# A hybrid decoder layer on one core: conditioning in whole, evenly spaced visits, and an instruction order planned by a simulated timeline

## The chip, the cores and the metric

The kernel runs on one core of one Trainium2 chip. The metric is device time in microseconds (us) of one execution. The times of before are 1353.8, 1354.12 and 1354.7 us, with a median of 1354.12.

TensorE (PE in the profile; PEld is its loading of weights), VectorE (DVE), ScalarE (ACT) and GpSimd (POOL) each run their own instructions in order. SyncE (SP) issues nearly all loads from HBM, one after another in its own order.

## The reference

One decoder layer works on 256 prompt tokens of one request and on 8 requests of 4 sample tokens, 288 columns in all, of width D = 2048. Everything is fp32.

```
mod = silu(c) @ w_ada + b_ada            # one row per request: sh1, sc1, g1, sh2, sc2, g2
h = rmsnorm(x, norm1) * (1 + sc1) + sh1
u_pool, z, xbc, dt = split(h @ w_in)     # 512, 1536, 2560, 24
pool_out = pool_mixer(u_pool)            # trailing means over 2, 4, 8, 16 tokens, a linear map each
ssd_out = ssd_mixer(z, xbc, dt)          # causal conv, chunked scan over 24 heads, gate silu(z), norm
x = x + g1 * (concat(pool_out, ssd_out) @ w_out)
h = rmsnorm(x, norm2) * (1 + sc2) + sh2
gate, val = split(h @ w_up)              # 5504 each
x = x + g2 * ((silu(causal_conv3(gate)) * val) @ w_down)
y = rmsnorm(x, norm_f)
```

The outputs are y and the states (pool, conv, SSD, feed-forward) of both groups.

## The kernel before, in words

**Projections.** Activations lie transposed: 128 rows of features, 288 columns of tokens. Each 128x128 block of a weight is multiplied in three matmuls of 288 columns (lines 303, 304, 305): the high part of the weight by the high and by the low part of the activation, and the low part of the weight by the high part. The weights are fp32 in HBM. They come as chunks of mostly 512 KB into tiles named raw_... (`load`, line 270, on SP's queue). ScalarE casts the high part (whi, line 289), VectorE subtracts it to get the low part (wlo, line 291), and only then can the chunk's matmuls run.

**Stages.** (1) Up to about 18 us: the sums of squares of x, and the first group of the conditioning. (2) The xbc projection, in seven blocks of k-tiles and output columns (`BLOCKS`), so that work begins before all of the input's modulation is known. Between its chunks come *visits* of the conditioning for the first norm, groups g1 to g5 (matmul line 378, tiles raw_ada and adag): each computes the shift and scale of some k-tiles. A visit's result is copied by ScalarE (asb), transposed on TensorE (adat) and added to the bias by VectorE. (3) From about 185 us: the last xbc block, then the uz projection (the z and pool columns). Between its matmuls come the SSD and pooling work (conv, cumulative sums cse, cb, state products s and yo, the outputs y; generators pulled as `back`) and parts 2, 3 and 4 of the conditioning (g1, sh2, sc2). (4) The out projection (mm_out and mm_outp) with the residual and the squares for the second norm. (5) The second norm (ssum2, rstd2), the first up columns (mm_up), then 40 pairs of gate and val columns and the down projection; part 5 of the conditioning (g2) lies at its start. (6) The last norm and the stores of y.

**Conditioning in parts.** Part p is a product of the 9 conditioning rows, padded to 32, with a 2048x2048 piece of w_ada. `ada_part_units` loads two chunks per k-tile and issues two matmuls of 512 columns for each (line 332; the profile counts two passes for one such fp32 matmul). It yields after every chunk or every few. The loops of stages 3 and 4 advance it with `pull(adas, rate)` at fixed rates (`RA1`, `RA2`, `TA`, `ADA_OUT`, divided by `AY`), so that as a rule four chunks, eight program matmuls, come together.

**What sets the order.** The code is written with the framework's tile scheduler. It takes the instructions with their priorities (`tc.high_priority()`), tile buffers, and pins (`tc.keep_in_program_order`), and decides in which order they stand on each engine and queue, the loads on SP too. A stretch inside `in_order` (the beginning) keeps the written order. The raw tiles rotate through slots kept by the class `_W`: 8 in pool w0 and 8 in pool w1, all shared by conditioning and projections; w0 is dropped ahead of the last xbc block. `top_up` issues loads of the early stage ahead, as many as there are slots.

**Norms.** `final_sum` adds the last column sums (ssum2, line 241), ScalarE takes the square root and VectorE the reciprocal (r3rstd2, lines 247 and 248), TensorE spreads it over the partitions (pbrstd2, line 254), ScalarE copies it, VectorE and GpSimd modulate x, and ScalarE casts the first operand h2h for mm_up. The SSD output has the same chain as ysum and pbrstdy. In the order of before, matmuls of part 5 (`GA`) and of part 4 lie between the links.

**Other loads.** vec (constants per feature, 476 KB) is issued on SP when block 4 of xbc starts, the pool weights poolw (256 KB) in `late_loads`, and the SSD's old states h0 (profile rows h<-h) in the SSD part.

Of the kernel before, what the change touches and what calls it, by code (L numbers as in the profile page):

```python
# [12 lines left out]
F32 = mybir.dt.float32  # L13
# [26 lines left out]
RAW0, RAW1, RAW2 = 8, 8, 1  # L40
# [11 lines left out]
AY = 2  # L52

RA1, RA2, RB1, RB2, RB3 = 0.5, 0.4, 1.0, 1.0, 1.0
TA, ADA_OUT = 4, 4
# [109 lines left out]
def kernel(ctx: ExitStack, tc, ins, outs):  # L165
# [101 lines left out]
    def load(key):  # L267
        off, cols = S.items[key]
        t = wp[0].tile([P, RAWC], F32, tag="raw", name="raw_" + "_".join(map(str, key)))
        nc.sync.dma_start(t[:, :cols], wflat[off:off + P * cols].rearrange("(p n) -> p n", p=P))  # L270
        return t
# [5 lines left out]
    def top_up():  # L277

        while queue and nloads[0] - min((n for n, _ in ahead.values()), default=nloads[0]) < RAW0 + RAW1:
            key = queue.popleft()  # L280
            ahead[key] = (nloads[0], load(key))
            nloads[0] += 1
# [121 lines left out]

    def ada_part_units(part, ay=1):
# [8 lines left out]
        yield  # L414
        pt = ada_tr(asb, 512, f"p{part}")
        for i in range(4):
            o = ada[:, part].rearrange("p (j i) c -> p j i c", j=4)[:, :, i, :]
            b = bada[:, part].rearrange("p (j i) -> p j i", j=4)[:, :, i]
            src = pt[:, i * P:(i + 1) * P].rearrange("p (j c) -> p j c", j=4)[:, :, 0:NC9]
            nc.vector.tensor_tensor(o, src, b.unsqueeze(2).to_broadcast([P, 4, NC9]), ALU.add)  # L420
        if part == 4:
            ada_scale(1, 4, vec[:, V_N2:V_N2 + KT], 0, KT)
        yield
# [33 lines left out]
    class _W:  # L457


        def __init__(self):  # L460
            self.slots = {"raw": [], "whi": [], "wlo": []}
            self.i = {"raw": 0, "whi": 0, "wlo": 0}

        def add(self, pool, nraw, nsp):
            for tag, n in (("raw", nraw), ("whi", nsp), ("wlo", nsp)):
                m = len(self.slots[tag])
                if m:
                    r = self.i[tag] % m
                    self.slots[tag] = self.slots[tag][r:] + self.slots[tag][:r]
                    self.i[tag] = 0  # L470
                self.slots[tag] += [(pool, n)] * n

        def drop(self, pool):
            for tag, sl in self.slots.items():
                r = self.i[tag] % len(sl)
                self.slots[tag] = [x for x in sl[r:] + sl[:r] if x[0] is not pool]
                self.i[tag] = 0

        def tile(self, shape, dt, tag, name):
            pool, n = self.slots[tag][self.i[tag] % len(self.slots[tag])]  # L480
            self.i[tag] += 1
            return pool.tile(shape, dt, tag=tag, name=name, bufs=n)

    wp[0] = _W()
    wp[0].add(ctx.enter_context(tc.tile_pool(name="w1", bufs=1, side="right")), RAW1, SPLIT1)
# [16 lines left out]
    wp[0].add(w0, RAW0, SPLIT0)  # L502
# [405 lines left out]
    adas = chain(*(ada_part_units(p, AY) for p in (2, 3, 4)))  # L908
# [86 lines left out]
    for bi in range(len(BLOCKS)):  # L995
        last = bi + 1 == len(BLOCKS)
        top_up()
        if last:

            wp[0].drop(w0)  # L1000
            w0_ctx.close()
            sx[0] = mx_ctx.enter_context(tc.tile_pool(name="sx", bufs=1, reuse_waits="tile"))
            raw = load(("dt",))[:, :KT * NH].rearrange("p (k h) -> p k h", h=NH)
# [11 lines left out]
            late_states()  # L1015
            dt_stage(ps)
# [4 lines left out]
        for i, m in enumerate(xbc_units(bi)):  # L1021
# [9 lines left out]
            else:  # L1031
                pull(back, 0.5 if m < 20 else RB1) if m >= 9 else None
                pull(adas, RA1 / AY)
# [4 lines left out]
    for m in list(range(4 + 3 * ZEARLY, 16)) + ULATE:  # L1038
        for _ in uz_units(m):
# [3 lines left out]
            pull(adas, RA2 / AY)  # L1043
# [7 lines left out]
    pull(adas, TA / AY)  # L1051
# [36 lines left out]
    for i in range(KT // YK):  # L1088
# [6 lines left out]
        if i == 3:  # L1095
            psq = aux("ysum")
            col_sums(psq, ssq, ones[:, 0:1], True, True)
            _, rstdy = rstd_of(psq, NH * 64, "rstdy")
    mx_ctx.close()
# [51 lines left out]
    for m in range(16):  # L1151
# [3 lines left out]
        if m == 5:  # L1155
            wp[0].add(w2, RAW2, SPLIT2)
        if m == 0:
            out_norm(ps0[0], m)
        else:
            for i, (pz, pp) in enumerate(out_units(m)):  # L1160
                if m == KT - 1 and i == 5:
                    all_but_last("ssum2")
                if i == NZ // YK - 1:
                    out_norm(pz, m)
        residual(ps0[1] if m == 0 else pp, 2, m)
        squares(m, "a")
        pull(adas, (1 + (m >= 14 - ADA_OUT)) / AY)
# [3 lines left out]

    adag2 = ada_part_units(5)
# [285 lines left out]
```

## Time and profile before

| what | us |
|---|---|
| median of 3 runs | 1354.12 |
| the profiled execution's own time | 1353.11 |
| its span in the trace | 1351.3 |
| TensorE busy in it | 1337.3 |
| VectorE busy | 820.0 |
| ScalarE busy | 579.4 |
| GpSimd busy | 227.5 |

The page gives busy times and, in 40 slices of the span, the busy tenths of each engine and of the DMA engines. The windows view gives the same for stretches that one chooses, with the granted TensorE clock (PEclk, 1.00 is full speed), the share of the 16 DMA engines in use and GB/s. The waits view lists what an engine waited for. The timeline lists start, duration, engine, line and tiles; neighbours of one kind are put together (x16 is sixteen passes), and durations of matmuls overlap, so that the time between two starts tells more than a duration. A row of an issue names the queue (SPq) and the chunk's tile without its numbers.

### The profile page before, as it was taken

What the parts mean: (1) busy time and instruction counts of PE and PEld (TensorE: products, weight loads), DVE (VectorE), ACT (ScalarE), POOL (GpSimd) and SP (SyncE); (2) the same over time, 40 slices, a digit from 0 to 9 for tenths busy, and PEclk for the clock granted to TensorE, in tenths of its full rate; (3) what the DMA queues carried; (4) which work ended last, traced back from release to release, by engine and by line L of the source; (5) the groups of instructions that cost most, each with busy time, mean ns of one, the idle gap of its engine ahead of it and who ended that gap; (6) DMA issues with size and microseconds to landing.
All of it is one profiled execution on the core that took longest, in us unless ns stands there. A gap on an engine that the chain in (4) does not pass through costs nothing.

```text
span 1351.3 us, 26246 instructions
## 1 busy us (share of the span) xinstructions
PE 1337.3 (99%) x10517; PEld 1247.5 (92%) x10517; DVE 820.0 (61%) x1394; ACT 579.4 (43%) x911; POOL 227.5 (17%) x449
## 2 busy tenths in 40 slices
PE   9999999999999999999999999999999999999997
PEld 8889997776789889999999999999999999999997
DVE  5776568778665568645665445656655556566543
ACT  5343244587733335434443333434433343444442
POOL 0000012122122223111211001321120011132221
PEclk9999999999999999999999999999999999999999
DMA  9999768978888877787555555655555565566531
GB/s 373 405 408 368 252 242 324 340 257 295 324 332 323 320 253 257 249 280 265 181 187 182 162 178 183 204 183 196 181 180 164 184 191 184 187 207 194 179 119 70
DMA packets 97482, 323.19 MB, mean 239 GB/s; under 512 B 10768, under 2 KB 19920, under 8 KB 97360
## 3 DMA queue, kind: packets, MB, share of 16 engines
q1 hardware_dynamic: 93600, 310.79, 66.3%
q0 software_dynamic: 3184, 9.69, 2.0%
q8 instruction: 82, 1.34, 0.4%
q10 hardware_dynamic: 576, 1.03, 0.2%
q14 instruction: 40, 0.33, 0.1%
HBM read 309.78 MB, written 10.39 MB: 237 GB/s over the span
## 4 chain that ended last, share of the span: by engine, by line
PE 74%; DVE 1%; issue 0%; ACT 0%; DVEq 0%
PE mm_down L304 7%; PE mm_down L303 7%; PE mm_down L305 7%; PE mm_gate L303 6%; PE mm_val L304 6%; PE mm_gate L304 6%; PE mm_val L305 6%; PE mm_gate L305 6%; PE mm_val L303 6%; PE adap L332 3%; PE mm_out L303 2%; PE mm_out L304 2%; PE mm_out L305 2%; PE mm_up L303 1%; PE mm_up L304 1%; PE mm_up L305 1%
## 5 line engine op out<-in xcount | busy, mean ns | idle before, releaser
L304 PE MATMUL mm_down<-al,whi_down 128*128 128x288 f32 x688 | 202.5, 294 | 0.0
L303 PE MATMUL mm_down<-ah,whi_down 128*128 128x288 f32 x688 | 202.4, 294 | 0.0
L305 PE MATMUL mm_down<-ah,wlo_down 128*128 128x288 f32 x688 | 202.0, 294 | 0.0
L304 PE MATMUL mm_val<-h2l,whi_val 128*128 128x288 f32 x640 | 189.1, 296 | 0.0
L304 PE MATMUL mm_gate<-h2l,whi_gate 128*128 128x288 f32 x640 | 189.1, 295 | 0.0
L303 PE MATMUL mm_gate<-h2h,whi_gate 128*128 128x288 f32 x640 | 188.8, 295 | 0.0
L305 PE MATMUL mm_val<-h2h,wlo_val 128*128 128x288 f32 x640 | 188.4, 294 | 0.0
L305 PE MATMUL mm_gate<-h2h,wlo_gate 128*128 128x288 f32 x640 | 188.4, 294 | 0.0
L303 PE MATMUL mm_val<-h2h,whi_val 128*128 128x288 f32 x640 | 187.9, 294 | 0.0
L291 DVE TENSOR_TENSOR wlo_gate<-raw_gate,whi_gate 128x1024 fp32r<-128x1024 f32 x80 | 98.4, 1230 | 136.4 <-ACT whi_gate L289 136.3
L291 DVE TENSOR_TENSOR wlo_down<-raw_down,whi_down 128x1024 fp32r<-128x1024 f32 x96 | 107.5, 1120 | 116.9 <-ACT whi_down L289 114.4
L289 ACT CAST whi_down<-raw_down 128x1024 fp32r<-128x1024 f32 x96 | 92.3, 961 | 167.0 <-PE mm_down L304 118.0
L289 ACT CAST whi_gate<-raw_gate 128x1024 fp32r<-128x1024 f32 x80 | 83.8, 1049 | 160.0 <-PE mm_gate L304 64.9
L289 ACT CAST whi_val<-raw_val 128x1024 fp32r<-128x1024 f32 x80 | 84.1, 1051 | 119.5 <-issue 101.9
L303 PE MATMUL xbc<-h1h,whi_xbc 128*128 128x288 f32 x448 | 133.5, 301 | 0.8 <-ACT h1h L453 0.7
L304 PE MATMUL xbc<-h1l,whi_xbc 128*128 128x288 f32 x448 | 132.0, 296 | 0.0
L305 PE MATMUL xbc<-h1h,wlo_xbc 128*128 128x288 f32 x448 | 130.0, 295 | 0.0
L303 PEld LDWEIGHTS mm_down<-ah,whi_down 128*128 128x128 f32 x688 | 129.2, 188 | 0.0
L304 PEld LDWEIGHTS mm_down<-al,whi_down 128*128 128x128 f32 x688 | 129.1, 188 | 0.0
L305 PEld LDWEIGHTS mm_down<-ah,wlo_down 128*128 128x128 f32 x688 | 129.0, 187 | 0.0
L303 PEld LDWEIGHTS mm_gate<-h2h,whi_gate 128*128 128x128 f32 x640 | 120.3, 188 | 5.0 <-ACT ah L1221 3.4
L305 PEld LDWEIGHTS mm_gate<-h2h,wlo_gate 128*128 128x128 f32 x640 | 120.5, 188 | 0.0
(331 smaller groups left out, 2994.8 us busy)
## 6 DMA issues: line engine op xcount, KB each, us to landing
raw_adap<-wflat SPq DMA_DIRECT2D x128, 512.0 KB, 5.6
raw_gate<-wflat SPq DMA_DIRECT2D x80, 512.0 KB, 3.6
raw_val<-wflat SPq DMA_DIRECT2D x80, 512.0 KB, 3.9
raw_ada<-wflat SPq DMA_DIRECT2D x64, 512.0 KB, 9.6
raw_xbc<-wflat SPq DMA_DIRECT2D x50, 512.0 KB, 9.5
raw_down<-wflat SPq DMA_DIRECT2D x48, 512.0 KB, 3.6
raw_out<-wflat SPq DMA_DIRECT2D x32, 512.0 KB, 7.6
raw_down<-wflat SPq DMA_DIRECT2D x32, 384.0 KB, 3.1
```

The lines of the kernel that those rows point to most:

```text
L289: yield nc.scalar.copy(hi[:, :n], raw[:, a:a + n])
L291: yield hi, lo, nc.vector.tensor_tensor(lo[:, :n], raw[:, a:a + n], hi[:, :n].bitcast(F32), ALU.subtract)
L303: nc.tensor.matmul(ps, whi[:, w], bh, start=first, stop=False)
L304: nc.tensor.matmul(ps, whi[:, w], bl, start=False, stop=False)
L305: nc.tensor.matmul(ps, wlo[:, w], bh, start=False, stop=last)
L332: nc.tensor.matmul(ps[32 * j:32 * j + 32, :nb], sc_c[:, k, :], raw[:, c:c + nb], start=(k == 0), stop=(k == KT - 1), tile_position=(0, 32 ...
```

## The change

**1. Visits of a counted size at counted distances.** `ada_visits` takes the place of `ada_part_units` for parts 2, 3 and 4 (part 5 keeps it). A visit of parts 2 and 3 has `AK` = 2 k-tiles (four chunks, eight program matmuls); one of part 4 has `AK2` = 4 (eight chunks, sixteen program matmuls). A visit's chunks are loaded one visit ahead, and its matmuls go through them from the last loaded to the first, pinned together. The end of a part (`ada_end`: transposes, bias) comes with the next visit, and adds the bias in one VectorE operation where there were four. The loops advance the generator at rates counted from the number of steps (`VA`), and the out projection at steps 3, 6, 9 and 12 (`AOUT`).

**2. Slots.** The raw slots of pool w1 are split into 4 "raw" and 4 "rawa". All 16 are shared until the last xbc block; then rawa become a ring of their own for the conditioning parts, and return to the others ahead of part 5. One more raw slot comes from pool sx. `_W` keeps the rings with `turn`, `add`, `move`, `drop` and `ix`.

**3. The planned order.** The scheduler runs with `schedule_with_timeline_sim=True`: it decides the order on each engine and queue by a simulated timeline of the kernel.

```diff
-RAW0, RAW1, RAW2 = 8, 8, 1
+RAW0, RAW1, RAWA, RAW2 = 8, 4, 4, 4
-AY = 2
-
-RA1, RA2, RB1, RB2, RB3 = 0.5, 0.4, 1.0, 1.0, 1.0
-TA, ADA_OUT = 4, 4
+VA = (5.01 / 28, 11.01 / 62)
+AK, AK2, AOUT = 2, 4, (3, 6, 9, 12)
+
+RB1, RB2, RB3 = 1.0, 1.0, 1.0
...
+    def ada_visits(parts, step, spread=False):
+        plan = [(part, k0) for part in parts for k0 in range(0, KT, step)]
+        ahead, end = [], None
+        def chunks(v):
+            part, k0 = plan[v]
+            for k in range(k0, k0 + step):
+                for h in range(2):
+                    ahead.append((k, h, load(("adap", part, k, h), "rawa")))
+                    if spread:
+                        yield
+            if not spread:
+                yield
+                yield
+        yield from chunks(0)
+        for v, (part, k0) in enumerate(plan):
+            if end:
+                ada_end(*end)
+                end = None
+            if k0 == 0:
+                ps = pa.tile([P, 512], F32, tag="ada", name=f"adap{part}")
+            n = 0
+            for k, h, raw in ahead[::-1]:
+                for j in (2 * h, 2 * h + 1):
+                    with tc.high_priority() if n else nullcontext():
+                        i = nc.tensor.matmul(ps[32 * j:32 * j + 32, :], sc_c[:, k, :],
+                                             raw[:, 512 * (j % 2):512 * (j % 2) + 512], start=k == step - 1,
+                                             stop=k == KT - step, tile_position=(0, 32 * j))
+                    tc.keep_in_program_order(i)
+                    n += 1
+            ahead.clear()
+            if k0 + step == KT:
+                end = part, ada_sb(ps, 512, f"p{part}")
...
-    adas = chain(*(ada_part_units(p, AY) for p in (2, 3, 4)))
+    adas = ada_visits((2, 3), AK)
...
             late_states()
+            next(adas)
             dt_stage(ps)
...
-                pull(adas, RA1 / AY)
+                pull(adas, 4 * VA[0])
...
-            pull(adas, RA2 / AY)
+            pull(adas, 4 * VA[1])
...
+            adas = ada_visits((4,), AK2, True)
...
+                if i % 2 and m < AOUT[-1] and m % 3:
+                    next(adas)
...
-        pull(adas, (1 + (m >= 14 - ADA_OUT)) / AY)
+        if m in AOUT:
+            next(adas)
...
-    with _tile.TileContext(nc) as tc:
+    with _tile.TileContext(nc, schedule_with_timeline_sim=True) as tc:
```

**What the change moves.** SP's queue in the early stage, between the loads for xbc block 3 and those for block 4 (raw_ada_3 is the third group's conditioning, raw_xbc_3_2 the third chunk of block 3). Before:

```order
L270 DMA raw_xbc_3_1_790<-wflat 128x1024
L270 DMA raw_ada_3_12_792<-wflat 128x1024
L270 DMA raw_ada_3_13_794<-wflat 128x1024
L270 DMA raw_ada_3_14_822<-wflat 128x1024
L270 DMA raw_ada_3_15_850<-wflat 128x1024
L270 DMA raw_xbc_3_2_868<-wflat 128x1024
L270 DMA raw_xbc_3_3_870<-wflat 128x1024
L270 DMA raw_xbc_4_0_872<-wflat 128x1024
L270 DMA raw_xbc_4_1_874<-wflat 128x1024
```

And SP's queue now, at the same place:

```order
L270 DMA raw_xbc_3_1_790<-wflat 128x1024
L768 DMA h0_0_2_2944<-h0 128x2x384
L270 DMA raw_ada_3_12_792<-wflat 128x1024
L270 DMA raw_ada_3_13_794<-wflat 128x1024
L270 DMA raw_ada_3_14_822<-wflat 128x1024
L270 DMA raw_ada_3_15_850<-wflat 128x1024
L270 DMA raw_xbc_3_3_870<-wflat 128x1024
L270 DMA raw_xbc_4_0_872<-wflat 128x1024
L270 DMA raw_xbc_4_1_874<-wflat 128x1024
L270 DMA raw_ada_4_0_930<-wflat 128x1024
L270 DMA raw_xbc_3_2_868<-wflat 128x1024
```

An h0 load now stands among them, and raw_xbc_3_2 has gone back behind two later chunks of xbc block 4, one of block 3 and one of the conditioning's fourth group. Further ahead in the same queue, vec and poolw now stand in front of raw_ada_2_2, and two larger h0 loads in front of raw_ada_2_7 and behind raw_xbc_2_2; before, vec stood behind raw_xbc_4_7 and the others later still.

TensorE in the uz columns: the last visit of part 2 (adap2) beside SSD matmuls (y, and cse, which spreads the cumulative sums). Before:

```order
L332 MATMUL adap2_2518<-raw_adap_2_14_0_3273,sc_c_84 32x512 x2
L332 MATMUL adap2_2518<-raw_adap_2_14_1_3275,sc_c_84 32x512 x2
L332 MATMUL adap2_2518<-raw_adap_2_15_0_3281,sc_c_84 32x512
L821 MATMUL y0_0_3236<-e0_0_3186,xdt0_2982 64x32 x2
L824 MATMUL y0_0_3236<-e0_0_3186,xdt0_2982 64x128 x2
L827 MATMUL y0_0_3236<-e0_0_3186,xdt0_2982 64x128
L828 MATMUL y0_0_3236<-ec0_0_3187,s1_0_3112 64x128
L827 MATMUL y0_0_3236<-e0_0_3186,xdt0_2982 64x128
L828 MATMUL y0_0_3236<-ec0_0_3187,s1_0_3112 64x128
L332 MATMUL adap2_2518<-raw_adap_2_15_0_3281,sc_c_84 32x512
L332 MATMUL adap2_2518<-raw_adap_2_15_1_3283,sc_c_84 32x512 x2
L801 MATMUL cse4_3291<-csr_150,selr_149 128x288
```

TensorE's same visit now, with its neighbours in the uz stream:

```order
L305 MATMUL mm_uz_12_3530<-h1h2_119,wlo_uz_12_0_3535 128x288
L303 MATMUL mm_uz_12_3530<-h1h3_120,whi_uz_12_0_3533 128x288
L432 MATMUL adap2_2511<-raw_adap_2_15_1_3431,sc_c_84 32x512 x2
L432 MATMUL adap2_2511<-raw_adap_2_15_0_3429,sc_c_84 32x512 x2
L432 MATMUL adap2_2511<-raw_adap_2_14_1_3427,sc_c_84 32x512 x2
L432 MATMUL adap2_2511<-raw_adap_2_14_0_3425,sc_c_84 32x512 x2
L859 MATMUL cse7_3510<-csr_150,selr_149 128x288
L859 MATMUL cse8_3553<-csr_150,selr_149 128x288
L304 MATMUL mm_uz_12_3530<-h1l3_136,whi_uz_12_0_3533 128x288
```

The group of y matmuls that stood inside the visit is elsewhere; the eight matmuls follow one another.

TensorE at the second norm, with part 5 of the conditioning (adap5). Before:

```order
L332 MATMUL adap5_6020<-raw_adap_5_1_1_6031,sc_c_84 32x512 x2
L241 MATMUL ssum2_5979<-ones_71,sqa_15_6005 128x1 x3
L332 MATMUL adap5_6020<-raw_adap_5_2_0_6049,sc_c_84 32x512
L254 MATMUL pbrstd2_6043<-early_69,r3rstd2_6040 128x128 x2
L254 MATMUL pbrstd2_6043<-early_69,r3rstd2_6040 128x32
L332 MATMUL adap5_6020<-raw_adap_5_2_0_6049,sc_c_84 32x512
L332 MATMUL adap5_6020<-raw_adap_5_2_1_6051,sc_c_84 32x512 x2
L332 MATMUL adap5_6020<-raw_adap_5_3_0_6057,sc_c_84 32x512 x2
L332 MATMUL adap5_6020<-raw_adap_5_3_1_6059,sc_c_84 32x512 x2
L332 MATMUL adap5_6020<-raw_adap_5_4_0_6065,sc_c_84 32x512 x2
L332 MATMUL adap5_6020<-raw_adap_5_4_1_6067,sc_c_84 32x512 x2
L303 MATMUL mm_up0_6105<-h2h0_6073,whi_upk0_6010 128x288
```

TensorE there now:

```order
L332 MATMUL adap5_6011<-raw_adap_5_3_1_6050,sc_c_84 32x512 x2
L332 MATMUL adap5_6011<-raw_adap_5_4_0_6056,sc_c_84 32x512 x2
L332 MATMUL adap5_6011<-raw_adap_5_4_1_6058,sc_c_84 32x512 x2
L241 MATMUL ssum2_5970<-ones_71,sqa_15_5996 128x1 x3
L254 MATMUL pbrstd2_6034<-early_69,r3rstd2_6031 128x128 x2
L254 MATMUL pbrstd2_6034<-early_69,r3rstd2_6031 128x32
L303 MATMUL mm_up0_6096<-h2h0_6064,whi_upk0_6001 128x288
```

The twelve matmuls of part 5 that stood behind ssum2, in two gaps of the norm's chain, stand ahead of it.

## What was predicted

> **What bounds the kernel now.** I began with the page: span, busy time and the slices of the DMA engines.
>
> ```profile
> span 1351.3 us, 26246 instructions
> PE 1337.3 (99%) x10517; PEld 1247.5 (92%) x10517; DVE 820.0 (61%) x1394; ACT 579.4 (43%) x911; POOL 227.5 (17%) x449
> DMA  9999768978888877787555555655555565566531
> ```
>
> TensorE is busy for 99% of the span, so the kernel can only become faster through fewer or cheaper TensorE instructions. A reordering has at most the idle remainder to win. It can lose more than that, because any wait on TensorE goes straight to the end. The third row says where a wait could come from: the DMA engines are full in the first four slices and never again. So next I read the windows view for TensorE, cut by stage.
>
> ```profile
> core 0: us, PE busy (x), PEclk, DMA share, GB/s
> 18.00:70.00 52.00, 51.44 (x583) 1.00 1.03 406
> 70.00:110.00 40.00, 40.00 (x358) 1.00 1.03 408
> 110.00:185.00 75.00, 75.00 (x662) 1.00 0.79 282
> 185.00:380.00 195.00, 192.29 (x1496) 1.00 0.82 300
> 500.00:1340.00 840.00, 840.00 (x6347) 1.00 0.59 191
> ```
>
> From 18 to 110 us TensorE is full and the DMA engines are full as well (share 1.03, 406 to 408 GB/s). Nothing is to spare there: bytes put in front of a load make it late. From 110 us on there is room. The stage from 500 us on, 840 us of feed-forward, has no idle time, and the order of TensorE's instructions in it is nearly the same after the change, so I leave it at its old time. The waits view of TensorE shows all that there is to win by better order:
>
> ```profile
> PE cse L801 <- DVE ada L420: 1.0, 1, 1.0
> PE pool L888 <- DVE pout L883: 0.8, 1, 0.8
> PE dttr L582 <- DVE dtt L570: 0.6, 1, 0.6
> PE cb L751 <- DVE xde L740: 0.3, 1, 0.3
> ```
>
> Together 2.7 us.
>
> **The change, part by part.** *1. Loads put ahead in the full stretch.* The planned order puts vec, poolw and three loads of h0 (the rows h<-h, two large, one small) among the conditioning and xbc loads, and four xbc and conditioning chunks ahead of raw_xbc_3_2. Sizes from the table of DMA issues:
>
> ```profile
> vec<-vec SPq DMA_DIRECT2D x1, 476.0 KB, 10.1
> poolw<-pool_w SPq DMA_DIRECT2D x1, 256.0 KB, 2.9
> h<-h SPq DMA_DIRECT2D x8, 576.0 KB, 6.5
> h<-h SPq DMA_DIRECT2D x4, 384.0 KB, 6.5
> ```
>
> That is 476 + 256 + 2 x 576 + 384 = 2268 KB, plus 4 x 512 = 2048 KB, in all 4316 KB. At 408 GB/s these take 4316 x 1024 / 408,000 = 10.8 us. In the old order raw_xbc_3_2 is the first of four issues in the first row below; the second gives the time from issue to landing of such loads, then follow its cast on ScalarE, the first matmul that uses it and a transpose beside it.
>
> ```profile
> 59.14 4.12 SPq L270 DMA_DIRECT2D raw_xbc<-wflat  x4
> ```
> ```profile
> DMA to landing us min/median/max: 9.0/10.2/10.4
> ```
> ```profile
> 69.42 1.05 ACT L289 CAST whi_xbc<-raw_xbc 128x1024 fp32r<-128x1024 f32 x1 [5.36 <-PE xbc L305]
> ```
> ```profile
> 71.13 0.40 PE L303 MATMUL xbc<-h1h,whi_xbc 128*128 128x288 f32 x1
> 71.69 0.44 PE L343 MATMUL adat_g<-early,asb_g 128*128 128x128 f32 x2
> ```
>
> So it lands at 59.14 + 10.2 = 69.3, is cast by 70.5 and is used at 71.13: a margin of 0.7 us. After the change it lands at 69.3 + 10.8 = 80.1 and is cast by 81.2. By the new order TensorE has done 12 more 288-column matmuls and a transpose before it needs that chunk. A 288-column matmul takes 840 / 6347 = 0.13 us in the last stage of the windows view, so with 12 x 0.13 and some 0.3 us for the transposes (the last row above and its switch) it would come there at 73.0. It waits 81.2 - 73.0 = 8.2 us, in pieces: the displaced loads are spread, so the conditioning chunks behind the first 576 KB (raw_ada_2_7) are late already. The visit of conditioning that follows needs chunks that land another 0.3 us too late. I take **+8.5 us**. Nothing covers it: TensorE works in order, and the work behind cannot step forward. The bounds are 0, if the displaced bytes found room, and 10.8, all of them unhidden; the rows say that there is neither room nor much slack, so I stay near the upper end. What is removed later in exchange is worth nothing, since from 110 us on the DMA engines were not the limit.
>
> The Trainium skill, "DMA: Bandwidth & Descriptors", section "Where 436 GB/s comes from", says that loads from HBM are held to about 358 GB/s per core; this trace has 406 to 408 GB/s and disagrees. By the skill's figure the same bytes would take 12.3 us and the wait would be 9.7 us, an estimate.
>
> *2. Whole visits.* A visit of conditioning leaves the stream of 288-column matmuls and comes back. First a whole visit of eight program matmuls (two passes each), then one that the old order cuts in two around a group of SSD matmuls, both from TensorE's timeline:
>
> ```profile
> 566.63 0.29 PE L305 MATMUL mm_val<-h2h,wlo_val 128*128 128x288 f32 x1
> 566.86 1.92 PE L332 MATMUL adap<-raw_adap,sc_c 128*32 128x512 f32 x16
> 568.71 0.40 PE L303 MATMUL mm_gate<-h2h,whi_gate 128*128 128x288 f32 x1
> 568.95 0.30 PE L304 MATMUL mm_gate<-h2l,whi_gate 128*128 128x288 f32 x1
> ```
> ```profile
> 262.85 1.90 PE L332 MATMUL adap<-raw_adap,sc_c 128*32 128x512 f32 x10
> 264.68 0.31 PE L821 MATMUL y<-e,xdt 128*64 128x32 f32 x4
> ...
> 265.66 1.06 PE L332 MATMUL adap<-raw_adap,sc_c 128*32 128x512 f32 x6
> 266.65 0.53 PE L801 MATMUL cse<-csr,selr 128*128 128x288 f32 x2
> ```
>
> Whole: 568.71 - 566.86 = 1.85 us. Cut: (264.68 - 262.85) + (266.65 - 265.66) = 1.83 + 0.99 = 2.82 us. A cut costs 0.97 us. The old order cuts six visits of parts 2 to 4 that the new one leaves whole (four by SSD groups, one into one and seven matmuls, one around the pool and ysum matmuls); the new one cuts one around the yo matmuls. The visit around dttr is cut in both. Net five, **-4.8 us**. Bounds: 0, if the SSD matmuls left alone pay as much for their own entry, and 6 x 0.97 = 5.8.
>
> *3. Part 4 in four visits of sixteen instead of eight of eight.* From the view of the conditioning tiles, the weight loads:
>
> ```profile
> L332 PEld LDWEIGHTS adap<-raw_adap,sc_c x424: 106/109/110, 196.0 to 499.9; 128*32 128x32 f32 x142
> ```
>
> From L305 to L304 the whole visit above takes 2.32 us, less 2 x 0.13 for the two pitches 2.06; sixteen passes at 0.109 us are 1.74, so entering and leaving costs 0.32. Four visits fewer give 4 x 0.32 = **-1.3 us**. Against it, two early visits of sixteen stand as four of eight in the new order: 2 x 0.32 = **+0.6 us**. The one vector operation in place of four at a part's end is off the path: VectorE is busy for 61%.
>
> *4. Filling around rstd2.* The norm ahead of the feed-forward is a chain through ScalarE and VectorE. In the old order conditioning part 5 lies in both of its gaps, by the chain that ended last:
>
> ```profile
> 495.72 0.76 PE ssum L241 x6
> 496.48 0.97 PE adap L332 x2
> 497.45 0.79 PE pbrstd L254 x6
> 498.24 2.71 PE adap L332 x22
> ```
> ```profile
> 496.81 0.18 DVE L248 RECIPROCAL r3rstd<-r3rstd 128x3 f32<-128x3 f32 x1 [2.10 <-ACT r3rstd L247]
> ```
>
> In the new order all twenty program matmuls of that piece stand ahead of ssum2, and ssum2, pbrstd2 and mm_up follow one another. Their work is only moved, so both gaps become idle time. The first is as long as the chain: the reciprocal ends at 496.99, so pbrstd could start about 0.55 us after ssum's end. The second lasts until h2h is cast, 2.71 us. **+3.3 us**, between 0 (if the cast came at once) and 0.97 + 2.71 = 3.7.
>
> *5. ysum.* The same happens at the norm of the SSD output: in the new order adat_p3, ysum and pbrstdy stand together behind a visit, where the old one had fourteen passes between the last two. The wait is at most the 0.97 us above for the norm, and about 0.4 for the copy that adat_p3 needs, since a copy of 256 columns takes 0.37 us:
>
> ```profile
> 71.27 0.37 ACT L337 COPY asb_g<-adag 128x256 f32<-128x256 f32 x1 [0.80 <-PE adag L378]
> ```
>
> **+1.4 us**, bounds 0 and 1.4.
>
> *6. Old waits.* The new order has SSD matmuls 20 to 100 matmuls later behind what they read; of the 2.7 us I take half away: **-1.3 us** (0 to -2.7).
>
> Sum: 8.5 + 0.6 - 4.8 - 1.3 + 3.3 + 1.4 - 1.3 = **+6.4 us**. The profiled execution took 1353.1 us (span 1351.3 and 1.8 around it): 1359.5. The median of the runs shown, 1354.1, is 1.0 above that execution, so I forecast **1360.5 us**. Up from there: all 10.8 us unhidden (+2.3) and half the gain of whole visits gone (+2.4), 1365. Down: the cast and the old margin hidden (-1.8), half of rstd2's second gap filled (-1.4) and all old waits gone (-1.4), 1356.
>
> **The rivals.** *A: the early loads are hidden.* For it: the raw weights have sixteen slots before and after, so if SP's queue ran further ahead of TensorE than it does now, h0 and vec would cost nothing. Against it: the share of 1.03 and the margin of 0.7 us. The point from which it decides: raw_xbc_3_2 landing before about 74 us. Then 8.5 falls to about 0 and the sum is 6.4 - 8.5 = -2.1 us: **1352 us**, faster or not to be told from before. If half the gap at rstd2 went too, 1350.5.
>
> *B: gaps slow TensorE beyond their length.* At the start its matmuls run at half pace:
>
> ```profile
> 1.06 6.17 PE L229 MATMUL warm<-ones 128*128 128x128 f32 x28 [1.06 <-DVE ones L194]
> ```
> ```profile
> 16.20 1.56 PE L229 MATMUL warm<-asb_g,ones 128*128 128x128 f32 x12
> ```
>
> 28 passes in 6.17 us are 0.22 each against 1.56 / 12 = 0.13 later, so a cold start cost about 28 x 0.09 = 2.5 us. If the waits of parts 1 and 4 come in pieces long enough to cool the array, three such restarts add 7.5: **1368 us**. Against it: every row of the windows view grants 1.00, and the waits of before, up to 1.0 us, left no trace in it. The Trainium skill, "TensorE: Matmul & The Clock Gate", section "HAM oscillation", gives this rule: an idle time beyond about 3.4 us halves the clock until it has been busy as long again. No run here has such a wait after the start.
>
> *C: the change does not do what it says.* The visits are whole in the order but gain nothing on the chip, because what stands beside them pays the switch; then -4.8 becomes 0 and the time is 1365 us.
>
> **How the numbers follow.** Forecast 0.56, A 0.20, B 0.17, C 0.07. The forecast's own range is 1356 to 1365. For 8 in 10 I take it whole, most of A from 1351 up, C, and half of B: **1351 to 1370 us**. A measurement can tell about 0.2%, 2.7 us: faster is below 1351.4, slower above 1356.8. Half of A and a little of what lies outside the cases gives faster 0.12; the other half of A and the forecast's lower edge gives within 0.12; the rest, 0.76, is slower.
>
> **What would show it.** The waits view of TensorE should have xbc and adag waiting for DMA or for ScalarE's cast between 35 and 90 us, some 8 us in all, and TensorE's busy share in 18 to 110 us should fall accordingly. Around rstd2 TensorE should idle once for 0.5 us and once for nearly 3 us. The stage of the uz columns should be some 4 us shorter, and the feed-forward as long as before, with a granted clock of 1.00. If raw_xbc_3_2 is used without a wait, A is right; if the clock's row dips after a gap, B; if the uz stage is not shorter, C. Waits of SSD matmuls of several us each would make the whole wrong.

## The result and the profile after

The changed kernel takes 1387.65 us (median of 4 runs, 1386.5 to 1389.8) where the one before takes 1354.22 in the same runs: a ratio of 1.0253, 95% interval 1.0241 to 1.0266. That is 33.4 us more. The direction was forecast, the size was not: 6.4 us were expected and the range ended at 1370.

The page of the changed kernel begins with these rows:

```profile
span 1386.7 us, 26255 instructions
PE 1346.7 (97%) x10517; PEld 1259.6 (91%) x10517; DVE 829.2 (60%) x1382; ACT 591.6 (43%) x919; POOL 227.3 (16%) x449
```

TensorE runs the same 10517 instructions and is busy for 9.4 us longer, in a span that is 35.4 us longer. So most of the loss is idle time, but some of it is work that runs slower. The windows view by stage shows both; the columns are TensorE's busy time, granted clock, DMA share and GB/s, and stages 3 and 4 end later than before:

```profile
18.00:70.00 52.00, 45.58 (x483) 0.91 1.03 403
70.00:110.00 40.00, 35.84 (x323) 0.95 1.02 404
...
185.00:400.00 215.00, 205.64 (x1607) 0.98 0.71 258
400.00:520.00 120.00, 114.46 (x853) 0.96 0.91 334
```

The clock was 1.00 in every one of these stretches before. Now it falls to half behind TensorE's longer waits. These are the longest of them; before, only the start's 1.1 us for warm reached more than 1.0 us:

```profile
PE xbc L303 <- ACT whi_xbc L289: 7.5, 2, 4.2
PE y L875 <- ACT ec L865: 6.9, 2, 3.8
PE adap L432 <- DMA raw_adap<-wflat: 2.5, 1, 2.5
PE adag L378 <- DMA raw_ada<-wflat: 2.5, 1, 2.5
PE pbrstdy L254 <- DVE r3rstdy L248: 2.3, 1, 2.3
PE mm_up L303 <- ACT h2h L499: 2.2, 1, 2.2
```

In all TensorE waits some 30 us where it waited 4.5. The clock records of the trace have it at half for 37.5 us ahead of the kernel's end, 4.2 of them idle, so half pace cost about (37.5 - 4.2) / 2 = 16.7 us. The added waits, 26 us, and the pace make 42 us, and the span grew by 35; that the 7 us between them are what the whole visits save is argued by subtraction only.

Where on the way the time is lost is read from TensorE's timeline, by the start of three landmarks (us):

| kernel | mm_dt (end of the early xbc blocks) | mm_up (behind the second norm) | ssumf (last norm) |
|---|---|---|---|
| before | 185.4 | 500.9 | 1336.8 |
| after | 201.8 | 533.9 | 1372.4 |

So 16.4 us go before mm_dt, 16.6 between mm_dt and mm_up, 2.5 in the feed-forward.

**The early 16.4 us.** The three long waits ahead of mm_dt, from TensorE's timeline:

```profile
42.62 3.05 PE L378 MATMUL adag<-raw_ada,sc_c 128*32 128x128 f32 x64 [2.47 <-DMA raw_ada<-wflat]
64.98 0.61 PE L303 MATMUL xbc<-h1h,whi_xbc 128*128 128x288 f32 x1 [3.29 <-ACT whi_xbc L289]
87.36 0.40 PE L303 MATMUL xbc<-h1h,whi_xbc 128*128 128x288 f32 x1 [4.16 <-ACT whi_xbc L289]
```

The first is raw_ada_2_7, behind the first h0 load that was put ahead; the second is a chunk of block 2 that lands at 64.1; the third is raw_xbc_3_2. SP issues that one as the first of four, and the tile's view gives the longest time to landing:

```profile
70.33 4.17 SPq L270 DMA_DIRECT2D raw_xbc<-wflat  x4
```
```profile
DMA to landing us min/median/max: 6.7/9.6/10.2
```

It lands at 70.33 + 10.2 = 80.5, where the prediction said 80.1. But its cast starts only at 86.26, since ScalarE's planned order has the modulation and the casts of the next operand ahead of it:

```profile
82.35 2.08 ACT L488 ACTIVATE h_g<-h_g,ada,amul 128x256 f32<-128x256 f32 x4 [1.52 <-DVE amul L347]
84.33 1.03 ACT L289 CAST whi_xbc<-raw_xbc 128x1024 fp32r<-128x1024 f32 x1
85.26 1.09 ACT L499 CAST h1h<-h_g 128x288 fp32r<-128x288 f32 x3
86.26 1.99 ACT L289 CAST whi_xbc<-raw_xbc 128x1024 fp32r<-128x1024 f32 x2
```

And behind each wait TensorE runs at half pace for a while. Behind the third:

```profile
87.00:90.00 3.00, 2.65 (x12) 0.61 1.02 408
90.00:93.00 3.00, 3.00 (x21) 0.82 1.03 410
```

The three waits are 2.5 + 3.3 + 4.2 = 10.0 us. The clock records have TensorE at half for 13.7 us before mm_dt, 1.2 of them idle, so the pace cost (13.7 - 1.2) / 2 = 6.2 us. Together they are the 16.4 us but for 0.2.

### The profile page after: what moved, and what is told of

It is laid out like the page before. It is cut to its first block, busy times and chain, and to the rows that moved or that the text cites. A ratio compares the mean times of both kernels' runs of the same rounds, so it can differ in the third digit from the quotient of the medians.

```text
span 1386.7 us, 26255 instructions
## 1 busy us (share of the span) xinstructions
PE 1346.7 (97%) x10517; PEld 1259.6 (91%) x10517; DVE 829.2 (60%) x1382; ACT 591.6 (43%) x919; POOL 227.3 (16%) x449
## 4 chain that ended last, share of the span: by engine, by line
PE 91%; DMA 4%; ACT 3%; DVE 2%; issue 0%; SPq 0%; POOL 0%; DVEq 0%; ACTq 0%; POOLq 0%
PE mm_down L304 7%; PE mm_down L303 7%; PE mm_down L305 7%; PE mm_gate L303 6%; PE mm_val L304 6%; PE mm_gate L304 6%; PE mm_val L305 6%; PE mm_gate L305 6%; PE mm_val L303 6%; PE xbc L303 4%; PE xbc L304 4%; PE xbc L305 4%; PE adap L432 3%; PE mm_out L303 2%; PE mm_out L304 2%; PE adag L378 2%
```

## The experiments

The kernel before ran beside each experiment. Ratios are to it, with 95% intervals.

### The visits without the planned order

```diff
-    with _tile.TileContext(nc, schedule_with_timeline_sim=True) as tc:
+    with _tile.TileContext(nc) as tc:
```

> The changed kernel with the framework's default order instead of the planned one: visits and rings alone. Theory 1 (the loss lies in the planned order: waits of TensorE and the half pace behind them; the visits themselves save what their rows say): clearly below the kernel before, about 1349 us (1346 to 1352), no wait of TensorE over 1.5 us and a granted clock of 1.00 in all stretches. Rival (the evenly spread visits and the split rings of raw tiles starve other work, whoever orders it): 1365 us or more, with waits for raw_adap or raw_xbc in the waits view.

Measured: 1357.43 us beside 1353.28, ratio 1.0034 (1.0021 to 1.0048). Neither theory's number. Up to ysum the visits do what their rows say: it starts at 371.6 us instead of 380.2. The time away from the 288-column stream between mm_dt and mm_up (for each stretch the time from the last such matmul to the next, less one pitch) falls from 108.3 us in 72 stretches to 103.2 in 62, 5.1 us. But then the out projection waits:

```profile
PE mm_out L303 <- ACT whi_out L289: 3.3, 2, 2.0
PE mm_out L305 <- DVE wlo_out L291: 2.7, 3, 1.5
```

With the pace behind those waits, that costs some 9 us: the stretch from mm_dt to mm_up grew by 4.1 us in spite of the 5.1 saved. The visits are not free of loss, but they are not the 33 us.

### The planned order without the visits

```diff
-    with _tile.TileContext(nc) as tc:
+    with _tile.TileContext(nc, schedule_with_timeline_sim=True) as tc:
```

> The kernel before with the planned order and nothing else. Theory 1: nearly the whole loss, 1385 to 1395 us, with the xbc stage ending some 16 us later than before (mm_dt near 202 us) and waits for ec, pbrstdy and h2h as in the changed kernel. Rival (visits and rings): within 5 us of before, 1354 to 1360 us.

Measured: 1401.65 us, ratio 1.0356 (1.0341 to 1.0370): 48 us more, beyond what theory 1 gave. mm_dt starts at 201.5, as in the changed kernel, so the early loss belongs to the planned order alone. From mm_dt to mm_up it loses 29 us where the changed kernel loses 17: with the old visits in small units the plan cuts more of them (98 stretches away from the stream between mm_dt and mm_up, where before had 72 and the changed kernel has 61). So the two parts of the change are not additive: the pinned visits take back some 14 us of what the planned order costs.

### The early loads in the written order: a first try

```diff
+        i = nc.sync.dma_start(t[:, :cols], wflat[off:off + P * cols].rearrange("(p n) -> p n", p=P))
+        if key[0] in ("xbc", "ada"):
+            tc.keep_in_program_order(i)
...
+        tc.keep_in_program_order(nc.sync.dma_start(vec, ins["vec"]))
...
+        tc.keep_in_program_order(nc.sync.dma_start(poolw, ins["pool_w"]))
...
+            tc.keep_in_program_order(nc.sync.dma_start(t[:, 0:nb, :], ins["h0"][b0:b0 + nb, :, g, :].rearrange("b p n -> p b n")))
```

> The changed kernel, planned order, but the loads of xbc, ada, vec, poolw and h0 are held in the order in which they are written, on SP. Theory 1 (the early loss comes from loads put ahead in the full DMA stretch): mm_dt begins near 187 us instead of 202, no wait of TensorE over 1.5 us before it, time 1370 to 1374 us; what is lost later stays. Rival (the early loss comes from TensorE's own planned order, split visits and earlier use of chunks): mm_dt at 198 us or later and 1384 us or more.

Measured: 1393.12 us, ratio 1.0287 (1.0270 to 1.0303), slower than the changed kernel. Yet mm_dt starts at 185.7, so the early 16 us are gone as theory 1 said. The stretch from mm_dt to mm_up grew from 332 to 354 us. TensorE's waits there name the loads of the last xbc block and of the conditioning:

```profile
PE xbc L305 <- ACT whi_xbc L291: 9.7, 5, 5.7
PE adap L434 <- DMA raw_adap<-wflat: 7.2, 3, 5.7
```

The pins reached into the last block. There the h0 loads stand in SP's queue at fixed places, and they need tiles that the stages before still hold; that this is what stopped the queue is inferred. The next run only shows that it goes away without those pins.

### The early loads held back, nothing pinned behind them

```diff
+        if key[0] == "ada" or key[0] == "xbc" and key[1] < len(BLOCKS) - 1:
+            tc.keep_in_program_order(i)
...
+            if g == 0:
+                nc.gpsimd.tensor_copy(t[:, 0, 0:1], cvp[3][:, 4, 3:4])
             nc.sync.dma_start(t[:, 0:nb, :], ins["h0"]...)
...
+        nc.gpsimd.tensor_copy(poolw[:, 0, 0:1], cvp[3][:, 4, 3:4])
         nc.sync.dma_start(poolw, ins["pool_w"])
```

> The changed kernel, planned order, with the loads of xbc blocks 0 to 5, of ada and of vec in the written order, and with poolw and the first three h0 loads held back by a one-column copy that they have to follow; nothing is pinned behind them. Output unchanged. Theory 1: mm_dt begins near 186 us instead of 201.8, and what is lost later stays as it is (332 us from mm_dt to mm_up): 1370 to 1374 us. Rival (the early loads pay later: held back, they delay the SSD stage by as much): the stretch from mm_dt to mm_up grows by 10 us or more and the time stays above 1380.

Measured: 1372.25 us, ratio 1.0141 (1.0128 to 1.0155), 15.4 us below the changed kernel. mm_dt starts at 185.1, mm_up 332.7 us later. In the windows view TensorE has no idle time from 70 to 110 us again:

```profile
70.00:110.00 40.00, 40.00 (x365) 1.00 1.03 409
```

So the early loss comes from the order of the loads in the full DMA stretch.

### The early loads alone, in the kernel before

```diff
+            if key == ("ada", 2, 2):
+                nc.sync.dma_start(vec, ins["vec"])
+                nc.sync.dma_start(poolw_t[0], ins["pool_w"])
...
+    keys = list(queue)
+    keys.remove(("xbc", 3, 2))
+    keys.insert(keys.index(("ada", 4, 0)) + 1, ("xbc", 3, 2))
+    queue = deque(keys)
```

> The kernel before, default order, with two things moved on SP: vec and poolw ahead of raw_ada_2_2, and raw_xbc_3_2 behind raw_ada_4_0. 3292 KB stand ahead of raw_xbc_3_2 that did not, 8.3 us at 408 GB/s; TensorE does some 1.6 us more before it needs the chunk, and the old margin was 0.7. Theory 1: waits of about 6 us in all between 35 and 85 us, followed by one or two stretches of half pace at 1.7 us each, mm_dt near 193 us and 1360 to 1363 us. Rival A of the prediction (loads put ahead are hidden): mm_dt within 2 us of 185.4 and 1354 to 1356 us.

Measured: 1363.88 us, ratio 1.0080 (1.0064 to 1.0095), 10.4 us more and a little above what theory 1 gave, with mm_dt at 195.4. Rival A is out. The main wait and the pace behind it, from TensorE's timeline and the windows:

```profile
79.77 0.61 PE L311 MATMUL xbc<-h1h,whi_xbc 128*128 128x288 f32 x1 [4.36 <-ACT whi_xbc L297]
```
```profile
79.00:85.00 6.00, 4.43 (x17) 0.50 1.03 410
```

8.3 us of displaced bytes cost 10 us: TensorE waits 6.9 us longer up to mm_dt than before, less than the bytes' own length, and most of the rest is pace. This run leaves out the three h0 loads (1536 KB) and keeps the default order on ScalarE; how the 6 us up to the changed kernel's 16.4 divide between these two was not taken apart.

### How long a wait must be to slow TensorE

```diff
+    def gap(m):
+        pg = aux(f"gap{m}")
+        t = kp.tile([P, NS], F32, tag="rsd", name=f"gt{m}", bufs=2)
+        tc.keep_in_program_order(nc.tensor.matmul(pg[:, :NS], ones, ones[:, :NS], start=True, stop=True))
+        nc.vector.tensor_copy(t, pg[:, :NS])
+        for _ in range(GAPS[m]):
+            nc.gpsimd.tensor_copy(t, t)
+        tc.keep_in_program_order(nc.tensor.matmul(pg[0:NS, P:2 * P], t, ones, start=True, stop=True))
```

> The kernel before with seven waits put into the last, dense part of the down projection: TensorE waits for a chain of 1, 3, 5, 7, 9, 12 and 15 small GpSimd copies. Output unchanged. It measures how long a wait must be before the granted clock falls. Theory 1a (waits of more than about 2 us cool TensorE to half pace, as the changed kernel's rows suggest): the shortest two or three waits, up to about 1.8 us, leave the clock at 1.00; those of 2.3 us and more are followed by 3 to 6 us at 0.5, so each costs 1.5 to 3 us beyond its own length. Rival 1b (only waits beyond 3.4 us do that, by the rule of the Trainium skill, page TensorE: Matmul & The Clock Gate, section HAM oscillation): at most the longest two show it.

Measured, in one execution: seven waits of 1.75, 2.29, 3.47, 4.01, 4.55, 5.37 and 6.18 us, 27.6 in all; the time is 1396.78, 43.5 more than before. The first two of them, and the clock behind them:

```profile
1256.24 0.41 PE L1277 MATMUL gap<-ones,gt 128*32 128x128 f32 x2 [1.75 <-POOL gt L1276]
...
1270.39 0.41 PE L1277 MATMUL gap<-ones,gt 128*32 128x128 f32 x2 [2.29 <-POOL gt L1276]
```
```profile
1257.00:1260.00 3.00, 3.00 (x25) 1.00 0.61 181
1271.00:1274.00 3.00, 3.00 (x16) 0.60 0.40 150
1274.00:1277.00 3.00, 3.00 (x21) 0.83 0.00 0
```

Behind 1.75 us the clock stays; behind 2.29 it falls about a microsecond after work resumes, for some 3.4 us. All longer waits show it too; the two longest have it for about 7 us, from 1.4 us before work resumes. So half pace cost about 1.7 us behind the waits of 2.3 to 4.6 us. Rival 1b is out: 2.29 us was enough.

The second such run has seven waits near the border, by `GAPS = {1: 3, 3: 1, 5: 2, 7: 3, 9: 1, 11: 2, 13: 3}`.

> The kernel before with seven waits in the last down projection again, now all near the border seen in the first such run (1.75 us left the clock at 1.00, 2.29 us did not): chains of 3, 1, 2, 3, 1, 2 and 3 copies. Output unchanged. If the length alone decides with a border between, all waits over about 2.1 us are followed by some 3.3 us at half pace and all under 1.8 by none. If it depends on where the wait falls in time, equal lengths give different answers.

Measured, in one execution (1374.56 us): the waits are 1.75, 2.02 and 2.29 or 2.30 us. Those of 1.75 and 2.02 do not lower the clock here. Of the three of 2.3 us, two do not and one does; here are the second and the third:

```profile
1298.49 0.41 PE L1277 MATMUL gap<-ones,gt 128*32 128x128 f32 x2 [2.29 <-POOL gt L1276]
...
1340.12 0.41 PE L1277 MATMUL gap<-ones,gt 128*32 128x128 f32 x2 [2.29 <-POOL gt L1276]
```
```profile
1300.00:1302.00 2.00, 2.00 (x18) 1.00 0.29 117
...
1342.00:1344.00 2.00, 2.00 (x10) 0.50 0.03 8
```

Equal lengths, different answers: near the border it also matters where the wait falls in time. The clock records show how. Within each trace, all changes of the clock between full and half lie whole multiples of 3.41 us apart, on one grid, and what goes with a fall is the idle time inside one stretch of that grid. The two waits of 2.3 us without effect lie across an edge, with 1.5 + 0.8 and 0.8 + 1.5 us; the third has 2.1 us in one stretch. The Trainium skill, "TensorE: Matmul & The Clock Gate", section "What's actually happening", says that the activity window is free-running and does not start with the kernel's work; that would explain it, and these runs agree. Its length of wait, about 3.4 us, is too long for this case.

Two of the other runs show that a border by length alone is wrong on both sides. In the changed kernel the wait of 3.29 us that ends at 64.98 is followed by half pace. The run with ScalarE's tables in order (below) has a wait of the same length at the same place, which an edge cuts into 1.85 + 1.44 us, and the clock stays. First the changed kernel, then that run:

```profile
64.00:67.00 3.00, 2.02 (x8) 0.50 1.04 407
```
```profile
64.75 0.40 PE L303 MATMUL xbc<-h1h,whi_xbc 128*128 128x288 f32 x1 [3.29 <-ACT whi_xbc L289]
```
```profile
66.00:69.00 3.00, 3.00 (x41) 1.00 1.04 399
```

In the run with visits alone 1.98 us were enough, since all of it falls into one stretch:

```profile
387.28 0.40 PE L303 MATMUL mm_out<-mixh,whi_out 128*128 128x288 f32 x1 [1.98 <-ACT whi_out L289]
```
```profile
387.00:390.00 3.00, 2.26 (x10) 0.69 1.02 407
```

Among dense 288-column matmuls, the clock of these traces stayed with up to 1.85 us of idle time in a stretch and fell from 1.9 us on. Around the SSD work and the norms, with their small matmuls, less was enough, down to 1.3 us; why is open.

### The tables of ScalarE

```diff
+    for i in list(traced[n0:]):
+        if i.engine == nc.scalar.engine and getattr(i, "func", None) in (AF.Silu, AF.Exp, AF.Relu, AF.Ln):
+            if prev is not None:
+                tc.add_manual_dep(i, prev.name, mybir.DependencyInfo(
+                    mybir.DependencyClass.NoSync, mybir.DependencyReason.DATA), reason="in_order")
+            prev = i
```

> The changed kernel, planned order, with ScalarE's Silu, Exp, Relu and Ln operations of the SSD stage in the order in which they are written; copies and casts stay free. The trace of the changed kernel has 23 table loads of 1.28 us between 185 and 385 us where the one before has 16 and the one with visits alone 12. Theory 1c (swapping tables makes ec and e late, and TensorE waits for them): table loads fall to about 16, the waits of y for ec from 6.9 us to under 2, and the time by 7 to 11 us to about 1378. Rival (ec is late because TensorE's planned order asks for it too early or because casts stand ahead of it): the waits stay and the time is 1385 us or more.

The reason for this run is ScalarE's timeline of the changed kernel, ahead of the y matmuls that wait 3.79 us for ec; their row on TensorE stands last:

```profile
307.82 1.28 ACT L754 ACT_TABLE_LOAD   x1
309.12 0.35 ACT L754 ACTIVATE cf<-cf 128x160 f32<-128x160 f32 x1
309.37 0.79 ACT L864 ACTIVATE e<-cse,csd 128x128 f32<-128x128 f32 x3
310.18 1.28 ACT L866 ACT_TABLE_LOAD   x1
311.47 0.68 ACT L866 ACTIVATE e<-e 128x576 f32<-128x576 f32 x1
312.06 0.26 ACT L865 ACTIVATE ec<-cse 128x128 f32<-128x128 f32 x1
```
```profile
312.37 0.41 PE L875 MATMUL y<-vec,yo 128*128 128x32 f32 x2 [3.79 <-ACT ec L865]
```

A Silu of the convolution stands between two groups of exponentials and costs two loads, 2.6 us. Measured: 1383.39 us, ratio 1.0224 (1.0210 to 1.0238), 4.3 us less than the changed kernel and between the two theories. Table loads fall from 28 to 20 in the whole run, as many as before the change, and y's waits for ec from 6.9 to 0.7 us. (Between 185 and 385 us they fall from 23 to 15; the run with visits alone has 14 there by its trace, not the 12 of the expectation.) But other waits grow, ysum's norm first:

```profile
PE pbrstdy L254 <- DVE r3rstdy L248: 4.8, 1, 4.8
PE y L875 <- ACT ec L865: 0.7, 1, 0.7
```

So the cause of the wait for ec is shown. Of the 6.2 us of waits that go, part comes back at the next late places. Not all of the 4.3 us is due to the tables either: in the traces mm_dt already starts 1.6 us earlier, with nearly the same waits ahead of it but less half pace, by the edge shown above.

### Part 5 around the second norm

```diff
+    with in_order(nc.tensor.engine):
+        for _ in range(GA[0]):
+            next(adag2)
+        rstd2p, rstd2 = final_sum("ssum2", "rstd2")
+        for _ in range(GA[1]):
+            next(adag2)
```

> The changed kernel, planned order, with TensorE's instructions around the second norm in the written order: twelve matmuls of part 5 stand between pbrstd2 and mm_up again, eight ahead of ssum2. Theory 1: the wait of mm_up for h2h, 2.2 us, goes, and with it the half pace in the first 6 us of the up columns (about 1.7 us): 1383 to 1385 us. Rival (part 5 only moved, so the place of the matmuls is worth nothing): 1387 to 1388 us.

Measured: 1385.36 us, ratio 1.0233 (1.0219 to 1.0247), 2.3 us under the changed kernel and just above what theory 1 gave. The intervals of the two kernels overlap, so the time alone does not prove the gain. The traces do show its two parts: mm_up starts 1.6 us earlier, and ssumf 3.2 us earlier, so another 1.6 us are won behind mm_up, where the half pace stood. The changed kernel at this place:

```profile
530.87 0.82 PE L254 MATMUL pbrstd<-early,r3rstd 128*128 128x128 f32 x6 [0.66 <-DVE r3rstd L248]
533.92 1.10 PE L303 MATMUL mm_up<-h2h,whi_upk 128*128 128x288 f32 x6 [2.23 <-ACT h2h L499]
534.82 0.44 PE L304 MATMUL mm_up<-h2l,whi_upk 128*128 128x288 f32 x1
```

And with part 5 back in the gap, where the same matmul takes 0.30 instead of 0.44 us:

```profile
529.59 2.78 PE L332 MATMUL adap<-raw_adap,sc_c 128*32 128x512 f32 x24
532.30 1.06 PE L303 MATMUL mm_up<-h2h,whi_upk 128*128 128x288 f32 x6
533.20 0.30 PE L304 MATMUL mm_up<-h2l,whi_upk 128*128 128x288 f32 x1
```

### Three repairs at once

The edits of three runs above together, in the planned order: loads held back, tables in order, part 5 around the norm.

> The changed kernel, planned order, with three repairs at once: the early loads held (-15.4 us alone), Silu, Exp, Relu and Ln in the written order (-4.3 alone), part 5 around the second norm (about -4 alone). If the causes are separate the sum holds: 1364 us (1361 to 1367). If the plan gives back what one repair gains, as when the loads were pinned with h0 among them, 1370 us or more.

Measured: 1360.53 us, ratio 1.0055 (1.0042 to 1.0069), a little below the expected span: the three take 27.1 us where their single gains sum to 15.4 + 4.3 + 2.3 = 22.0. So some 27 of the 33 us go with these three repairs together; the 5 us beyond the single gains are not taken apart. Of the 7 us that are left over the kernel before, the visits alone cost 4.1 in the default order (1357.43), and the waits for whi_out sum to 3.3 us here as there; that the two are the same loss is argued and not tested.

### The out projection

In the run with visits alone the out projection had 4 raw slots to itself, where before it shared 8 with the conditioning. Two tries:

```diff
-            for tag, n in (("rawa", RAW2), ("whi", SPLIT2), ("wlo", SPLIT2)):
-                wp[0].add(w2, tag, tag, n)
-            adas = ada_visits((4,), AK2, True)
+            for ring, tag, n in (("raw", "rawa", RAW2), ("whi", "whi", SPLIT2), ("wlo", "wlo", SPLIT2)):
+                wp[0].add(w2, ring, tag, n)
+            adas = ada_visits((4,), AK2)
```

> The visits with the framework's default order (as in the run with visits alone), but in the out projection part 4 goes in eight visits of eight matmuls, evenly spread, and the four raw slots of pool w2 belong to the projection's ring, which then has eight instead of four. If the waits for whi_out and wlo_out (6 us and two stretches at half pace) come from the short ring, they vanish, and whole visits show their saving of some 5 us: 1348 to 1350 us, faster than before. If they come from the visits' place or from something else, the time stays at 1356 us or more.

Measured: 1355.37 us, ratio 1.0012 (1.0004 to 1.0021): better than with the short ring, not what was expected. One wait of 2.5 us for whi_out is left. The second try gives up the visits and the split for part 4:

```diff
-RAW0, RAW1, RAWA, RAW2 = 8, 4, 4, 4
+RAW0, RAW1, RAWA, RAW2 = 8, 4, 4, 1
...
+        if m == 0:
+            wp[0].move("rawa", "rawa", "raw")
+            adas = ada_part_units(4, 2)
...
+        pull(adas, 10 / 14)
```

> Default order, whole visits for parts 2 and 3 only. The out projection is as before: all raw slots shared from its start, part 4 in eight visits of eight at the ends of the column blocks. With visits alone, ysum began at 371.6 us instead of 380.2, and the out projection then lost 10 us to waits for raw_out. If that loss belongs to the split ring and the planned visits of part 4, the gain of 8.6 us up to ysum stays, less the two visits of part 4 that the old order had done by then (2 x 2.0): 1348 to 1350 us. If the out projection waits here too, 1353 us or more.

Measured: **1349.87 us, ratio 0.9974 (0.9963 to 0.9984)**, 0.3% faster than the kernel before. mm_up starts at 497.9 instead of 500.9. For the out projection TensorE's waits view has one wait of 0.7 us for wlo_out and one of 0.6 for whi_out left, and the clock stays at 1.00.

So whole visits for parts 2 and 3, with their ring, in the default order are worth 3.6 us. Which of the two, the ring or the visits' places, starved the out projection was not taken apart further.

## Why the prediction was right or wrong

**Step 1, loads put ahead: right in mechanism, half in size.** The chunk landed at 80.5 (forecast 80.1), raw_ada_2_7 was late, and holding the loads back gave 15.4 us. The term said +8.5. The waits themselves came to 10.0 us, near the term. Most of what was missing is the half pace behind each of the three waits, 6.2 us in all, which the term put at nothing. And the path to the operand was misread: the chunk had landed 5.8 us before its cast began, because ScalarE's planned order had other work ahead of it. I read SP's and TensorE's order, and took the cast to follow the landing.

**Steps 2 and 3, whole visits: right in sum.** Forecast -4.8, -1.3 and +0.6; with visits alone the time away from the stream between mm_dt and mm_up fell by 5.1 us. That fits the cost per cut, though in another order than the one forecast, and no single cut was measured again. What I did not price is what carrying them costs: the out projection lost some 9 us to waits and pace in the default order, by the short ring or by the visits' places.

**Step 4, second norm: right in size, without the pace.** The visits ending at mm_up, ssum2 included, take 10.8 us where they took 7.8: +3.1 for a forecast of +3.3. The pace behind it, some 1.6 us, came on top.

**Step 5, ysum: too small.** Forecast +1.4. The stretch around pool, ysum and pbrstdy takes 12.5 us; before, its contents stood in two stretches of 4.9 and 2.4. That is +5.3: the norm's 2.3 us are not the 0.97 that I took from the second norm, since ScalarE has a cast and a table load of 1.28 us ahead of the square root, and a chunk of conditioning was 2.5 us late, which the term did not consider.

**Step 6, old waits: wrong in sign.** I gave -1.3 for SSD work that stands later. The old waits did vanish, but y and cse now wait 7.8 us for ec. I looked at distances on TensorE and not at what stands in ScalarE's queue ahead of ec; the tables there are the cause, by the run that orders them. The prediction's own sign that the whole is wrong, waits of SSD matmuls of several us each, came here: y waited 3.8 and 3.1 us.

**Rival B, waits that slow TensorE beyond their length, is what came true beside the forecast**, and I gave it 0.17 as an alternative instead of a factor on every wait. It had three restarts and 7.5 us; the trace has the clock at half in eight places ahead of the end, for about 17 us of loss. Its objection, that the waits of before left no trace in the clock, was sound only for waits up to 1.1 us. The rule of 3.4 us in the Trainium skill ("TensorE: Matmul & The Clock Gate", section "HAM oscillation") kept its chance low. Here a wait of 2.23 us ahead of mm_up slowed what followed. Rival A fell by the run with the early loads alone.

The step that failed is thus the pricing of waits in the sum. Its four terms for waits, 8.5 + 3.3 + 1.4 - 1.3 = 11.9 us, came from the orders of SP and TensorE alone, and the sum put the pace behind a wait at nothing. The trace has 26 us more waiting than before, the larger part of the excess where ScalarE's queue made an operand late (ec, r3rstdy), and about 17 us of pace.

## What to carry to other kernels

When an order is replanned, compare the queue of every engine that feeds the critical one, ScalarE's casts and table swaps too: a landed load is not a ready operand. Price a wait of TensorE at its length, and at 1.7 us more where it can put about 1.9 us of idle time into one 3.41-us stretch: in these runs a wait from 2 to 3.3 us did so or not by where it fell, one of 3.47 us or more always did. Where the DMA engines are full, look at every load that moved forward, whatever it is for: bytes ahead of a needed chunk came back as waits of nearly their length (6.9 us for 8.3, and 10.0 for 10.8), and then as pace.

## What the runs showed that I had not expected

- Length alone does not decide whether a wait lowers the clock: 1.98 us did in one run and 2.02 did not in another, 2.3 us did in two of four cases, 3.29 us did in one run and not in another, 3.47 us and more always did. The half pace begins and ends on a grid of 3.41 us that does not follow the waits, and lasts 3.41 us or a multiple of it.
- A table load on ScalarE takes 1.28 us, and the planned order brought 28 of them where the default one had 20 with the old visits and 18 with the new.
- The two halves of the change do not add up: +4.1 us for the visits alone, +48.4 for the planned order alone, +33.4 for both.
